# A two-block transformer on one core: engine orders from a planner of its own in place of the framework's

## The chip, the cores and the metric

The kernel runs on one core of one Trainium2 chip. A core has five instruction queues that run beside one another: TensorE (PE) for matmuls and transposes, ScalarE (ACT), VectorE (DVE), GpSimd (POOL), and SyncE (SP), which here only issues DMA transfers. Each queue is issued in the order in which the program was written out; semaphores hold an instruction back until what it needs is there. The metric is the time of one execution on the device in microseconds (us). Before the change the median of three runs is 2193.63 us (2193.45 to 2198.98).

## The reference

One sequence of 256 rows of width 1024 goes through two blocks of two layers each. All inputs are fp32.

```python
# first block, per layer
y = hybrid_mixer(x, ...)          # h = x @ w_in; three 8-head attentions (relative bias; low rank + rope; forgetting)
x = layer_norm(alpha*x + y)       # branches gated: sum_n sigmoid(g_n) * (y_n @ w_branch[n]), then @ w_out
y = memory_cross_attention(x, mem, ...);   x = layer_norm(alpha*x + y)
y = (silu(x @ w_g) * (x @ w_u)) @ w_down;  x = layer_norm(alpha*x + y)
# second block, per layer; nine vectors per layer from mod = silu(c) @ w_mod + b_mod
x = x + 0.5*g1 * swiglu(rms(x)*(1+sc1) + sh1)
x = x + g2 * mixer2(rms(x)*(1+sc2) + sh2)  # stick-breaking + dilated attention + gated linear recurrence (HGRN)
x = x + 0.5*g3 * swiglu(rms(x)*(1+sc3) + sh3)
```

The hidden width of every swiglu is 2816. Nearly all of the work is the product of 256 rows with some 300 MB of weights, read once.

## The kernel before

The 256 rows are two tiles of 128 (`t` = 0 and 1), written as two Python generators, `thread(0)` and `thread(1)`. `run` steps tile 0 until it asks for a weight, loads and splits that weight once (`weight`, L204 to L216), and hands it to tile 1 `lag` weights later. So the two tiles use the same weight a few us apart.

A weight chunk is 128x1024 fp32 (512 KB). SP loads it into one of 3 `raw` buffers (L209). ACT rounds each half to fp32r, `hi` (L214); DVE computes `lo = raw - hi` (L215). Both go into rings of 7 buffers, `wh` and `wl`, or into spare `E` buffers. Each product is three fp32r matmuls of 128x128 by 128x512 in `mm3` (L222 to L224): `xh*wh`, `xl*wh`, `xh*wl`. `wide` accumulates a group in PSUM pool `m`, one bank per tile; `narrow`, scores, transposes and the rest use pool `a`, three banks per tile. A group may start only when ACT or DVE has emptied its bank.

Results pass through small chains: transposes on PE (`blocks_T`, L267), the split of the transposed tile on ACT and DVE (L260, L261), softmax (L404 to L420: scores, row maximum on DVE, exponentials on ACT, reciprocal and product on DVE, then transposes and `values`, L391), the silu product of the FFN (L352, L353), the gate sums out of bank `m` (L539), the branch sum on GpSimd (L554), the layer norms (L289 to L296) and `modulated` with its squares on ACT (L305) and its scaling on DVE (L313). Attention is a generator beside the weights' stream (`beside`), pushed on one step per weight (`pump`).

The vectors `mod` of the second block are matrix-vector products without PE: 288 loads of 128x512 (256 KB) into 2 `mr` buffers (L753), each followed by one DVE multiply-and-sum (L754). `run` sprinkles them over the first block.

What sets the order: instructions are traced in program order, and the framework's scheduler puts each engine's into the order that is issued, by its own cost model, and gives each tile a buffer of its pool. The only hints are the lags above and `exp_next` (L171), which loads ACT's exp table right behind the last silu or sigmoid of a stage. [...]

Of the kernel before, what the change touches and what calls it, by code (L numbers as in the profile page):

```python
# [9 lines left out]
F32 = mybir.dt.float32  # L10
F32R = mybir.dt.float32r
U8 = mybir.dt.uint8
AF = mybir.ActivationFunctionType
# [103 lines left out]

class Program:
    def __init__(self, ctx, tc, io, out, probes=None):
        self.tc, self.nc, self.io, self.out, self.probes = tc, tc.nc, io, out, probes
        pool = lambda n, b, **k: ctx.enter_context(tc.tile_pool(name=n, bufs=b, **k))
# [22 lines left out]
    def tile(self, tag, shape, dt=F32):  # L147
        self.n += 1
        tag = tag if tag in self.pools else f"{tag}{self.t}"
        return self.pools[tag].tile(shape, dt, tag=tag if tag != "c" else f"c{self.n}", name=f"{tag}_{self.n}")  # L150

    def const(self, shape, ap, dt=F32):
        t = self.tile("c", shape, dt)
# [9 lines left out]
    def row(self, ap, n=D, tag=None):  # L163

        self.n += 1
        pool = self.pools["c" if tag else "bc"]
        t = pool.tile([128, n], F32, tag=tag or "bc", name=f"row_{self.n}")
        self.nc.sync.dma_start(t, ap.partition_broadcast(128))
        return t

    def exp_next(self, after):  # L171

        self.behind(self.nc.scalar.preload_act_table_set("natural_log_exp_and_others"), after)

    def behind(self, later, earlier):

        self.tc.add_manual_dep(later.ins, earlier.ins.name, mybir.DependencyInfo(
            mybir.DependencyClass.NoSync, mybir.DependencyReason.SCHED_ONLY), reason="order")

# [158 lines left out]
    def ffn(self, x, gu, dn, exps=False):  # L338

        nc = self.nc  # L340
        acc, todo = None, None
        ng = FH // 256

        def down(h, j):
            yield from self.narrow(h, range(2), dn[j * 256:j * 256 + 256], acc, j == 0, j == ng - 1)

        for j in range(ng):
            if self.t == 0:
                self.spare, self.deep, self.lag = True, NE, DEEP
            ps = yield from self.wide(x, gu[j], 512, 2)  # L350
            a = self.tile("T", [128, 512])
            silu = nc.scalar.activation(a[:, :256], ps[:, :256], AF.Silu)  # L352
# [9 lines left out]
        if self.t and exps:  # L362
            self.exp_next(silu)
        return acc


# [157 lines left out]
    def mixer(self, l, t, xT):  # L524
# [7 lines left out]
        def gates(n):  # L532
            if t == 0:
                st["bg", n] = self.row(io["b_gate"][l, n])
            out = []
            for h in range(2):
                ps = yield from self.wide(xT, main[6 + 2 * n + h], 512, 2)
                g = self.tile("S", [128, 512])
                nc.vector.tensor_tensor(g, ps, st["bg", n][:, h * 512:h * 512 + 512], op=ALU.add)  # L539
                out.append(g)  # L540
            for g in out:
                last = nc.scalar.activation(g, g, AF.Sigmoid)
            self.exp_next(last)
            return out

        def branch(n, y, gs):
# [54 lines left out]
        v = self.tile("S", [128, 8, 64])  # L601
# [329 lines left out]
    def mixer2(self, l, t, xT):  # L931
# [48 lines left out]
        def group(n):  # L980
            ps = yield from self.wide(xT, w[n], 512, 2)
            if n == 3:
                st["qs", t] = self.tile("T", [128, 512])
                silu = nc.scalar.activation(st["qs", t], ps, AF.Silu)
                if t:
                    self.exp_next(silu)
            elif n == 4:
                tasks["h"] = self.beside(hgrn_all(st["qs", t], ps))
                self.pump()
            elif n == 1:  # L990
                nc.scalar.copy(v2[:, :256], ps[:, :256])
                qd = self.normed_heads(t, ps[:, 256:], st["qg"])
                self.queries(t, self.blocks_T(qd, 2), 2, 4)
            elif n == 2:
                nc.scalar.copy(v2[:, 256:], ps[:, 256:])
                kd = self.normed_heads(t, ps[:, :256], st["kg"])
                nc.scalar.copy(k2[:, 256:], self.blocks_T(kd, 2)[:, :256])
                tasks["d"] = self.beside(dilated())
            elif n == 0:
                p = self.blocks_T(self.copied(ps), 4)  # L1000
                self.queries(t, p, 2, 0)
                nc.scalar.copy(k2[:, :256], p[:, 256:])
                tasks["s"] = self.beside(sticks())
            elif n == 5:
                st["ih", t] = self.copied(ps, "S")
            else:
                gs = self.tile("S", [128, 512])
                silu = nc.scalar.activation(gs, ps, AF.Silu)
                if t == 0 or ORDER[-1] != 6:
                    self.exp_next(silu)  # L1010
# [107 lines left out]
    def run(self, until=None):  # L1118

        self.setup()  # L1120
        ahead, behind = self.thread(0), self.thread(1)
        queue, count, passed, seen = deque(), 0, 0, 0

        def step(g, v):
            self.t = int(g is behind)
            try:
                return g.send(v)
            except StopIteration:
                return None
            finally:  # L1130
                self.t = 0

        want = step(ahead, None)
        other = None

        def follow(n):
            nonlocal other, seen
            while other is not None:
                if other[0] == "sync" and seen < passed:
                    seen += 1  # L1140
                    other = step(behind, None)
                elif other[0] == "w" and len(queue) > n:
                    ap, w = queue.popleft()
                    assert str(other[1]) == str(ap)
                    other = step(behind, w)
                else:
                    break

        while want is not None and (until is None or count < until):
            if want[0] == "sync":  # L1150
                follow(0)
                passed += 1
                want = step(ahead, None)
                continue
            w = self.weight(want[1], want[2])
            if want[0] == "w":
                queue.append((want[1], w))
            if count == 1:
                other = step(behind, None)
            if count == 8:  # L1160
                self.setup_later()
            want = step(ahead, w)
            follow(self.lag)
            count += 1
            if self.spare:
# [36 lines left out]
```

## Time and profile before

| | |
|---|---|
| median of 3 runs | 2193.63 us (2193.45 to 2198.98) |
| profiled execution | 2197.66 us, its span 2195.9 us |
| granted TensorE clock, mean | 0.996 |
| PE busy | 2105.4 us (96%), 10246 matmul records |
| DVE busy | 1576.0 us (72%) |
| ACT busy | 1232.5 us (56%) |
| DMA | 443.19 MB, 202 GB/s over the span |

Times in the views count from the start of the span. A matmul's record lasts about 0.39 us, longer than the distance to the next one's start, since matmuls are pipelined; so a PE that shows as busy can still be losing time. An idle stretch in a timeline stands in brackets, with the instruction that ended it. "PE a L267 <- DVE T L353" in the waits reads: a transpose of line 267 into pool `a` waited for the DVE instruction of line 353.

### The profile page before, as it was taken

Reading aid. Unit: us, or ns where it says so; the run is one execution under the profiler, and the core shown is the slowest. Engines: PE = TensorE matmul, PEld = TensorE weight load, DVE = VectorE, ACT = ScalarE, POOL = GpSimd, SP = SyncE. Lnnn points to the kernel's source line nnn. Section 1 sums busy time; section 2 is a strip of 40 time slices with the busy share of each in tenths; the row PEclk is TensorE's granted clock in tenths of the full one; section 3 lists DMA queues with packets and bytes.
Section 4 is the critical chain, followed back from the end, with each engine's and each line's share of the span. In section 5 each row is a group of like instructions: output and inputs, shape, how many; then the busy total and the mean of one; then the engine's idle time right before and its main releaser. Section 6 shows DMA issues by size and latency. Waiting matters only on the chain.

```text
span 2195.9 us, 29986 instructions
## 1 busy us (share of the span) xinstructions
PE 2105.4 (96%) x10246; PEld 1696.6 (77%) x10246; DVE 1576.0 (72%) x3245; ACT 1232.5 (56%) x2551; POOL 89.4 (4%) x120
## 2 busy tenths in 40 slices
PE   8999999999899999899999999999999999999999
PEld 6777777877778777788878877778887887777887
DVE  5788888777778888875585568985556556887554
ACT  5867645444476675544454446764445445776442
POOL 0000100000001011000010000000000000000000
PEclk9999999999999999999999999999999999999999
DMA  7677877888767778686656653455665665345663
GB/s 258 209 244 232 257 238 233 269 275 276 243 211 239 230 246 256 204 261 206 195 189 184 187 176 106 126 156 186 187 207 177 186 188 153 96 154 164 184 187 98
DMA packets 150320, 443.19 MB, mean 202 GB/s; under 512 B 19208, under 2 KB 24344, under 8 KB 150168
## 3 DMA queue, kind: packets, MB, share of 16 engines
q1 hardware_dynamic: 150168, 441.29, 64.2%
q8 instruction: 80, 1.31, 0.2%
q14 instruction: 72, 0.59, 0.1%
HBM read 440.10 MB, written 1.12 MB: 201 GB/s over the span
## 4 chain that ended last, share of the span: by engine, by line
PE 47%; DVE 6%; ACT 3%; DMA 2%; issue 1%; POOL 1%; POOLq 0%; ACTq 0%; DVEq 0%; SPq 0%
PE m L222 10%; PE m L223 10%; PE m L224 10%; PE a L222 5%; PE a L224 5%; PE a L223 5%; PE a L267 2%; DMA raw<-in_w_gu 1%; DVE wl L215 1%; PE a L871 1%; ACT wh L214 1%; DMA raw<-in_w_out 1%; ACT X L305 0%; POOL s L280 0%; DVE T L867 0%
## 5 line engine op out<-in xcount | busy, mean ns | idle before, releaser
L215 DVE TENSOR_TENSOR wl<-raw,wh 128x512 fp32r<-128x512 f32 (+1 forms) x982 | 654.3, 696 | 262.9 <-ACT wh L214 260.7
L214 ACT CAST wh<-raw 128x512 fp32r<-128x512 f32 (+1 forms) x982 | 568.4, 617 | 482.6 <-PE m L223 219.3
L222 PE MATMUL m<-wh,S 128*128 128x512 f32 (+2 forms) x1472 | 590.4, 401 | 20.6 <-DVE S L539 6.5
L223 PE MATMUL m<-wh,S 128*128 128x512 f32 (+2 forms) x1472 | 574.2, 390 | 3.5 <-DVE S L261 2.2
L224 PE MATMUL m<-wl,S 128*128 128x512 f32 (+2 forms) x1472 | 573.8, 391 | 0.4 <-DVE wl L215 0.4
L222 PEld LDWEIGHTS m<-wh,S 128*128 128x128 f32 x1472 | 278.6, 189 | 88.3 <-DVE S L539 9.3
L223 PEld LDWEIGHTS m<-wh,S 128*128 128x128 f32 x1472 | 279.3, 190 | 58.4 <-DVE S L325 3.9
L224 PEld LDWEIGHTS m<-wl,S 128*128 128x128 f32 x1472 | 278.0, 189 | 58.9 <-issue 2.2
L215 DVE TENSOR_TENSOR E<-raw,E 128x512 fp32r<-128x512 f32 x334 | 220.2, 687 | 123.1 <-ACT E L214 122.2
L214 ACT CAST E<-raw 128x512 fp32r<-128x512 f32 x334 | 196.0, 620 | 186.4 <-PE m L223 97.3
L754 DVE SCALAR_TENSOR_TENSOR mr<-mr,c 128x512 f32<-128x512 f32 x288 | 195.4, 689 | 108.8 <-DMA mr<-in_w_mod 107.9
L222 PE MATMUL a<-wh,S 128*128 128x512 f32 x472 | 188.8, 402 | 2.8 <-ACT S L260 2.8
L224 PE MATMUL a<-wl,S 128*128 128x512 f32 x472 | 185.9, 394 | 0.0
L223 PE MATMUL a<-wh,S 128*128 128x512 f32 x472 | 185.6, 393 | 0.0
L222 PE MATMUL m<-E,S 128*128 128x512 f32 x436 | 174.2, 400 | 0.7 <-ACT T L922 0.5
L223 PE MATMUL m<-E,S 128*128 128x512 f32 x436 | 171.8, 394 | 0.0
L224 PE MATMUL m<-E,S 128*128 128x512 f32 x436 | 171.7, 394 | 0.0
L260 ACT CAST S<-a 128x256 fp32r<-128x256 f32 (+2 forms) x200 | 85.7, 430 | 86.2 <-PE a L267 80.0
L267 PE MATMUL a<-c,T 128*128 128x128 f32 x652 | 112.2, 278 | 20.5 <-DVE T L353 6.8
L267 PEld LDWEIGHTS a<-c,T 128*128 128x128 f32 x652 | 81.2, 141 | 59.2 <-DVE T L353 12.5
L261 DVE TENSOR_TENSOR S<-a,S 128x256 fp32r<-128x256 f32 (+2 forms) x200 | 98.1, 492 | 37.8 <-ACT S L260 37.4
L222 PEld LDWEIGHTS a<-wh,S 128*128 128x128 f32 x472 | 88.5, 188 | 21.3 <-ACT S L260 3.7
(230 smaller groups left out, 2408.1 us busy)
## 6 DMA issues: line engine op xcount, KB each, us to landing
raw<-in_w_gu SPq DMA_DIRECT2D x264, 512.0 KB, 3.7
mr<-in_w_mod SPq DMA_DIRECT2D x288, 256.0 KB, 4.0
raw<-in_w_dn SPq DMA_DIRECT2D x132, 512.0 KB, 3.7
raw<-in_w_main SPq DMA_DIRECT2D x96, 512.0 KB, 4.3
raw<-in_w_in SPq DMA_DIRECT2D x56, 512.0 KB, 3.7
raw<-in_w_branch SPq DMA_DIRECT2D x24, 512.0 KB, 4.8
raw<-in_w_mo SPq DMA_DIRECT2D x16, 512.0 KB, 4.6
raw<-in_w_xkv SPq DMA_DIRECT2D x16, 512.0 KB, 4.3
```

Of the source, the lines that this page charges most:

```text
L214: nc.scalar.copy(hi[:, c], raw[:, c])
L215: nc.vector.tensor_tensor(lo[:, c], raw[:, c], hi[:, c], op=ALU.subtract)
L222: nc.tensor.matmul(ps, xh, wh, start=first, stop=False)
L223: nc.tensor.matmul(ps, xl, wh, start=False, stop=False)
L224: nc.tensor.matmul(ps, xh, wl, start=False, stop=last)
L260: nc.scalar.copy(h2, ps[:, :n])
L261: nc.vector.tensor_tensor(l2, ps[:, :n], h2, op=ALU.subtract)
L267: self.nc.tensor.transpose(ps[:, j * 128:(j + 1) * 128], src[:, j * 128:(j + 1) * 128], self.ident)
L754: nc.vector.scalar_tensor_tensor(raw, raw, 1.0, c[:, d], op0=ALU.mult, op1=ALU.mult, accum_out=m[:, k:k + 1])
L871: nc.tensor.matmul(ps[:, s], m[:, s], m[:, s], start=True, stop=True)
```

## The change

Every `nc.engine.op(...)` of the program now only records an `Op`: its engine, its data dependencies by tile and area, and a duration from a formula per engine and shape (`cost`). Pools are no longer the framework's: a `Tile` gets its place when its first instruction is placed. At the end `plan` does three things. First, each PE instruction gets as deadline (`late`) the sum of the PE durations in front of it in program order, and every other instruction the deadline of its earliest reader less its own duration and a hop; DMA gets 2500 ns and its bytes besides, and a tile that will be reused passes its next user's deadline back. Second, an event loop steps through time: a free engine takes the ready instruction with the smallest deadline, if its tiles have a free place. ACT passes over up to 11 instructions that need another function table, and loads a table when their deadline presses; `exp_next` goes away. A DMA is held until PE's progress is within 40 us of its deadline. Third, `emit` issues everything in that order, each tile at its planned place, with a semaphore on the last users of that place. The arithmetic, the tiles' sizes and the pools' counts stay.

```diff
+OVERLAP = {"PE": 0, "ACT": 95, "DVE": 83, "POOL": 0, "SP": 0}
+TABLE = 1300
+class Recorder:
+    def add(self, engine, name, args, kw):
...
+        op.dur, op.nbytes = self.cost(op, name, out[0], src, kw)
+        op.slot = max(op.dur - OVERLAP[op.eng], 40)
...
+    def cost(self, op, name, out, src, kw):
...
+        if op.eng == "PE":
+            return (4.7 + 0.4406 * n, 0) if src[1].dtype == F32R else ((1 if name == "transpose" else 2) * FP32, 0)
...
+    def plan(self):
...
+        for op in ops:
+            if op.eng == "PE":
+                op.late = total
+                total += op.slot
+        for op in reversed(ops):
+            lat = NEXT[op.eng]
+            for j in op.succ:
+                s = ops[j]
+                v = s.late - op.dur - (lat[s.eng] if s.eng != op.eng else 0)
+                if op.eng == "SP":
+                    v -= 2500 + op.nbytes / 200
+                if v < op.late:
+                    op.late = v
+            for j in reuse.get(op.i, ()):
+                if ops[j].i > op.i and ops[j].late - op.dur < op.late:
+                    op.late = ops[j].late - op.dur
...
+                    if x.eng == "SP" and early > progress:
+                        heapq.heappush(later, (early, x.i, x))
+                        continue
+                    heapq.heappush(ready[x.eng], (x.late, x.i, x))
...
+                    while q:
+                        k = heapq.heappop(q)
+                        if not room(k[2]):
+                            continue
+                        if e == "ACT" and k[2].set and table != k[2].set:
+                            held.append(k)
+                            if len(held) < 12:
+                                continue
+                            break
+                        op = k[2]
+                        break
+                    if held and (op is None or held[0][0] + TABLE < op.late):
...
+                    if e == "SP":
+                        dma = max(now + 1900, dma) + op.nbytes / 260
+                        end = dma
...
+    def emit(self, tc):
+        order, self.time = self.plan()
...
+        with tc.manual_schedule():
+            for n, op in enumerate(order):
+                while k < len(self.preload) and self.preload[k][1] <= n:
+                    self.nc.scalar.preload_act_table_set(self.preload[k][2])
...
+                ins = op.call(*args, **{a: real(v, op) for a, v in op.kw.items()})
...
 class Program:
-        self.tc, self.nc, self.io, self.out, self.probes = tc, tc.nc, io, out, probes
+        self.tc, self.nc, self.io, self.out, self.probes = tc, Recorder(tc.nc), io, out, probes
...
-    def exp_next(self, after):
-
-        self.behind(self.nc.scalar.preload_act_table_set("natural_log_exp_and_others"), after)
...
             for g in out:
-                last = nc.scalar.activation(g, g, AF.Sigmoid)
-            self.exp_next(last)
+                nc.scalar.activation(g, g, AF.Sigmoid)
...
         follow(0)
+        self.nc.emit(self.tc)
```

The orders below are each engine's, as issued. A name ends in a running number that differs between the two kernels; since every instruction is now issued by one line, the line says nothing after the change.

ScalarE at the first softmax of tile 0, before: `T_115` holds its scores, `wh_677` is a half of the next weight, `S_127` a value tile.

```order
L214 CAST wh_630<-raw_628 128x512 x2
L214 CAST wh_677<-raw_675 128x512
L415 ACT_TABLE_LOAD
L415 ACTIVATE T_115_570,s_117_572<-T_115_570,s_116_571 128x128 x4
L214 CAST wh_677<-raw_675 128x512
L450 COPY S_127_625<-m_101_505 128x512
L415 ACTIVATE T_123_607,s_125_609<-T_123_607,s_124_608 128x128 x4
L386 COPY T_134_648<-a_133_643 128x512
```

The same place after the change; here that weight is `wh_623`.

```order
L444 CAST wh_477<-raw_415 128x512
L440 ACT_TABLE_LOAD x2
L444 ACTIVATE T_115_532,s_117_572<-T_115_532,s_116_539 128x128
L444 CAST wh_578<-raw_461 128x512
L444 ACTIVATE T_115_532,s_117_572<-T_115_532,s_116_539 128x128
L444 CAST wh_578<-raw_461 128x512
L444 ACTIVATE T_115_532,s_117_572<-T_115_532,s_116_539 128x128
L444 COPY S_127_597<-m_101_437 128x512
L444 ACTIVATE T_115_532,s_117_572<-T_115_532,s_116_539 128x128
L444 CAST wh_607<-raw_474 128x512 x2
L444 ACTIVATE T_123_574,s_125_619<-T_123_574,s_124_611 128x128
L444 CAST wh_623<-raw_511 128x512
```

The rounding of that weight stood ahead of the exponentials, and now stands behind the four of `T_115`; the halves of an older weight, `wh_578`, stand between them, and two table loads in place of one in front.

TensorE at the same place, before: `a_133` takes the transposes of `T_115`, `m_110` is a group of tile 0, `m_128` one of tile 1.

```order
L223 MATMUL m_110_544<-wh_630,S_10_141 128x512
L224 MATMUL m_110_544<-wl_631,S_9_140 128x512
L267 MATMUL a_133_643<-c_117,T_115_570 128x128 x4
L222 MATMUL m_128_627<-wh_553,S_22_179 128x512
L223 MATMUL m_128_627<-wh_553,S_23_180 128x512
L224 MATMUL m_128_627<-wl_554,S_22_179 128x512
```

After the change:

```order
L444 MATMUL a_135_591<-S_99_435,E_142 128x128
L444 MATMUL m_110_501<-wl_586,S_9_173 128x512
L444 MATMUL m_128_605<-wh_452,S_22_196 128x512
L444 MATMUL m_128_605<-wh_452,S_23_205 128x512
L444 MATMUL m_128_605<-wl_466,S_22_196 128x512
L444 MATMUL m_128_605<-wh_452,S_22_196 128x512
L444 MATMUL m_128_605<-wh_452,S_23_205 128x512
L444 MATMUL m_128_605<-wl_466,S_22_196 128x512
L444 MATMUL a_135_591<-S_55_379,E_142 128x128
L444 MATMUL a_133_627<-c_131,T_115_532 128x128 x4
L444 MATMUL a_135_591<-S_99_435,E_142 128x128
L444 MATMUL m_110_501<-wh_607,S_9_173 128x512
```

The six matmuls of `m_128` stood behind the transposes and now stand ahead of them, with two score matmuls (`a_135`).

VectorE at the gates of layer 1 of the first block, before: `S_1350` is the gate sum that empties bank `m` of tile 1 (`m_1321`), `T_1343` a softmax, the `mr` rows are the sums for `mod`.

```order
L419 RECIPROCAL s_1329_5980<-s_1328_5979 128x2
L754 SCALAR_TENSOR_TENSOR mr_11396,c_3506<-mr_11396,c_3503 128x512
L420 TENSOR_TENSOR T_1326_5977<-T_1326_5977,s_1329_5980 128x512
L754 SCALAR_TENSOR_TENSOR mr_11419,c_10325<-mr_11419,c_3503 128x512
L404 SCALAR_TENSOR_TENSOR T_1343_6054<-a_1342_6049,E_5615 128x512
L754 SCALAR_TENSOR_TENSOR mr_11442,c_3506<-mr_11442,c_3503 128x512
L405 TENSOR_REDUCE s_1344_6055<-T_1343_6054 128x2
L539 TENSOR_TENSOR S_1350_6084<-m_1321_5951,row_5711 128x512
```

After the change:

```order
L444 SCALAR_TENSOR_TENSOR mr_6210,c_1090<-mr_6210,c_458 128x512
L444 SCALAR_TENSOR_TENSOR mr_6232,c_1101<-mr_6232,c_458 128x512
L444 TENSOR_TENSOR wl_6297<-raw_6196,wh_6291 128x512
L444 RECIPROCAL s_1329_6302<-s_1328_6286 128x2
L444 TENSOR_TENSOR T_1326_6244<-T_1326_6244,s_1329_6302 128x512
L444 TENSOR_TENSOR wl_6297<-raw_6196,wh_6291 128x512
L444 SCALAR_TENSOR_TENSOR T_1343_6317<-a_1342_6304,E_5592 128x512
L444 TENSOR_TENSOR wl_6324<-raw_6226,wh_6307 128x512
L444 TENSOR_REDUCE s_1344_6329<-T_1343_6317 128x2
L444 TENSOR_TENSOR wl_6324<-raw_6226,wh_6307 128x512
L444 TENSOR_TENSOR S_1350_6341<-m_1321_6219,row_5598 128x512
L444 SCALAR_TENSOR_TENSOR mr_6277,c_1090<-mr_6277,c_458 128x512
```

Three `mr` rows stood among the last seven ahead of the gate sum; now none stands among the last eight, and the nearest two come ahead of those.

ACT's function table is loaded 59 times in the order before, 47 times in the order after. The number of matmuls, transposes and transfers is the same.

## Rows read from the trace of the kernel before

**Rows 1.** Of the page: span, then engines with busy us, share of the span, instructions.

```profile
span 2195.9 us, 29986 instructions
...
PE 2105.4 (96%) x10246; PEld 1696.6 (77%) x10246; DVE 1576.0 (72%) x3245; ACT 1232.5 (56%) x2551; POOL 89.4 (4%) x120
```

**Rows 2.** Of the groups by shape on TensorE: busy us, mean ns | idle before.

```profile
L222 PE MATMUL m<-wh,S 128*128 128x512 f32 x1372 | 557.8, 407 | 17.6 <-DVE S L539 3.4 <-DVE S L324 2.8 <-ACT wh L214 2.7
...
L222 PE MATMUL a<-wh,S 128*128 128x512 f32 x472 | 188.8, 402 | 2.8 <-ACT S L260 2.8
...
L222 PE MATMUL m<-E,S 128*128 128x512 f32 x436 | 174.2, 400 | 0.7 <-ACT T L922 0.5 <-ACT T L450 0.2
...
L222 PE MATMUL a<-E,S 128*128 128x512 f32 x216 | 87.4, 405 | 0.0
...
L222 PE MATMUL m<-wh,S 128*128 128x256 f32 x68 | 19.8, 292 | 0.0
L222 PE MATMUL a<-wh,E 128*128 128x512 f32 x48 | 19.3, 402 | 0.5 <-ACT T L415 0.5
...
L222 PE MATMUL m<-wh,S 128*128 128x424 f32 x32 | 12.8, 400 | 3.0 <-DVE S L539 3.0
...
L222 PE MATMUL a<-E,E 128*128 128x512 f32 x16 | 6.2, 390 | 0.0
```

**Rows 3.** Of the timeline of TensorE, dense FFN: start us, us, what.

```profile
1714.79 0.39 PE L222 MATMUL m<-wh,S 128*128 128x512 f32 x1
...
1721.66 0.40 PE L222 MATMUL m<-wh,S 128*128 128x512 f32 x1
```

**Rows 4.** Of the timeline of TensorE, first softmax (idle before, releaser in brackets).

```profile
50.58 1.05 PE L377 MATMUL a<-S,E 128*128 128x128 f32 x8
...
58.47 0.72 PE L267 MATMUL a<-c,T 128*128 128x128 f32 x4 [4.06 <-DVE T L420]
```

**Rows 5.** Of the timeline of TensorE, the start.

```profile
4.13 1.94 PE L267 MATMUL a<-c,X 128*128 128x128 f32 x8 [4.13 <-DMA X<-in_x]
```

**Rows 6.** Of the timeline of TensorE, the end.

```profile
2190.80 0.40 PE L224 MATMUL a<-E,S 128*128 128x512 f32 x1
```

**Rows 7.** Of the stretches: us, then busy us of PE, PEld, DVE, ACT, POOL, clock, DMA.

```profile
660.00:935.00 275.00, 258.15 (x1381) 206.70 (x1381) 232.96 (x500) 169.66 (x356) 21.77 (x21) 1.00 0.74 236
...
1320.00:1485.00 165.00, 154.80 (x827) 124.27 (x826) 140.58 (x311) 114.38 (x256) 11.04 (x15) 0.99 0.44 133
1485.00:1650.00 165.00, 164.85 (x737) 133.78 (x735) 92.41 (x160) 80.75 (x162) 0.98 (x3) 1.00 0.63 192
```

**Rows 8.** Of the timeline of ScalarE, first softmax.

```profile
53.36 0.62 ACT L214 CAST wh<-raw 128x512 fp32r<-128x512 f32 x1 [6.50 <-DMA raw<-in_w_main]
53.99 1.28 ACT L415 ACT_TABLE_LOAD   x1
55.29 0.40 ACT L415 ACTIVATE T<-T,s 128x128 f32<-128x128 f32 x1
```

**Rows 9.** Of the timeline of VectorE, gates of layer 1.

```profile
645.03 0.69 DVE L754 SCALAR_TENSOR_TENSOR mr<-mr,c 128x512 f32<-128x512 f32 x1 [4.53 <-DMA mr<-in_w_mod]
```

**Rows 10.** Of the timeline of TensorE, gates of layer 1.

```profile
648.19 0.46 PE L222 MATMUL m<-wh,S 128*128 128x424 f32 x1 [3.03 <-DVE S L539]
```

**Rows 11.** Of the waits: engine, line, releaser: total us, times, longest.

```profile
DVE mr L754 <- DMA mr<-in_w_mod: 107.9, 97, 4.5
```

**Rows 12.** Of the waits of TensorE.

```profile
PE a L267 <- DVE X L313: 8.0, 10, 1.6
...
PE a L267 <- DVE X L296: 4.2, 5, 1.2
...
PE a L267 <- POOL X L554: 4.0, 4, 1.1
```

**Rows 13.** Of the page: DMA issues, KB each, median us to landing.

```profile
raw<-in_w_gu SPq DMA_DIRECT2D x264, 512.0 KB, 3.7
mr<-in_w_mod SPq DMA_DIRECT2D x288, 256.0 KB, 4.0
```

More of the change, by code (lines that the diff above doesn't have):

```diff
@@ L115, in _layout @@
     return {n: np.ascontiguousarray(a) for n, a in o.items()}
+SETS = {AF.Exp: "natural_log_exp_and_others", AF.Ln: "natural_log_exp_and_others", AF.Silu: "silu_and_others",
+        AF.Sigmoid: "sigmoid_and_others", AF.Sin: "trig_and_small"}
+NEXT = {
+    "PE": {"PE": 150, "ACT": 202, "DVE": 202, "POOL": 300, "SP": 300},
+    "ACT": {"PE": 55, "ACT": 0, "DVE": 32, "POOL": 100, "SP": 100},
+    "DVE": {"PE": 55, "ACT": 35, "DVE": 0, "POOL": 100, "SP": 100},
+    "POOL": {"PE": 60, "ACT": 40, "DVE": 35, "POOL": 0, "SP": 100},
+    "SP": {"PE": 135, "ACT": 95, "DVE": 95, "POOL": 130, "SP": 100},
+}
@@ new lines, with __init__, tile, __getattr__ @@
+class _Sketch:
+    def __init__(self):
+        import concourse.bacc as bacc
+        import concourse.tile as tile
+        self.nc = bacc.Bacc("TRN2", target_bir_lowering=False, num_devices=1)
+        self.tc = tile.TileContext(self.nc)
+        self.tc.__enter__()
+        self.pool = self.tc.alloc_tile_pool(name="sketch", bufs=1)
+    def tile(self, shape, dt, name):
+        return self.pool.tile(shape, dt, tag=name, name=name)
+class Engine:
+    def __init__(self, rec, real, name):
+        self.rec, self.real, self.name = rec, real, name
+    def __getattr__(self, op):
+        return lambda *a, **k: self.rec.add(self, op, a, k)
@@ L121, with pool @@
+FP32 = 110
 class Program:
     def __init__(self, ctx, tc, io, out, probes=None):
-        self.tc, self.nc, self.io, self.out, self.probes = tc, tc.nc, io, out, probes
-        pool = lambda n, b, **k: ctx.enter_context(tc.tile_pool(name=n, bufs=b, **k))
+        self.tc, self.nc, self.io, self.out, self.probes = tc, Recorder(tc.nc), io, out, probes
+        self.bufs = {}
+        def pool(n, b, **k):
+            self.bufs[n] = b
+            return ctx.enter_context(tc.tile_pool(name=n, bufs=1, **k))
@@ L149, in tile @@
         tag = tag if tag in self.pools else f"{tag}{self.t}"
-        return self.pools[tag].tile(shape, dt, tag=tag if tag != "c" else f"c{self.n}", name=f"{tag}_{self.n}")
+        return self.nc.tile(self.pools[tag], tag if tag != "c" else f"c{self.n}", self.bufs[tag], shape, dt, f"{tag}_{self.n}")
     def const(self, shape, ap, dt=F32):
@@ L166, in row @@
         pool = self.pools["c" if tag else "bc"]
-        t = pool.tile([128, n], F32, tag=tag or "bc", name=f"row_{self.n}")
+        t = self.nc.tile(pool, tag or "bc", 1 if tag else BUFS["bc"], [128, n], F32, f"row_{self.n}")
         self.nc.sync.dma_start(t, ap.partition_broadcast(128))
         return t
-    def exp_next(self, after):
-        self.behind(self.nc.scalar.preload_act_table_set("natural_log_exp_and_others"), after)
-    def behind(self, later, earlier):
-        self.tc.add_manual_dep(later.ins, earlier.ins.name, mybir.DependencyInfo(
-            mybir.DependencyClass.NoSync, mybir.DependencyReason.SCHED_ONLY), reason="order")
     def beside(self, gen):
@@ L351, in ffn @@
             a = self.tile("T", [128, 512])
-            silu = nc.scalar.activation(a[:, :256], ps[:, :256], AF.Silu)
+            nc.scalar.activation(a[:, :256], ps[:, :256], AF.Silu)
             nc.vector.tensor_tensor(a[:, 256:], a[:, :256], ps[:, 256:], op=ALU.mult)
@@ L361, in ffn @@
         yield from down(todo, ng - 1)
-        if self.t and exps:
-            self.exp_next(silu)
         return acc
@@ L983, in group @@
                 st["qs", t] = self.tile("T", [128, 512])
-                silu = nc.scalar.activation(st["qs", t], ps, AF.Silu)
-                if t:
-                    self.exp_next(silu)
+                nc.scalar.activation(st["qs", t], ps, AF.Silu)
             elif n == 4:
@@ L1007, in group @@
                 gs = self.tile("S", [128, 512])
-                silu = nc.scalar.activation(gs, ps, AF.Silu)
-                if t == 0 or ORDER[-1] != 6:
-                    self.exp_next(silu)
+                nc.scalar.activation(gs, ps, AF.Silu)
                 g3 = gs.rearrange("p (a b) -> p a b", a=4)
```

244 lines of the change are left out of this document (added).

## The prediction

> **What bounds the kernel now.** I read the page's busy times first. PE is busy 2105.4 of 2195.9 us, DVE and ACT far less [rows 1], so only PE's lost time can be won back by a new order. The page understates that loss, since a matmul's record overlaps the next one's. So I worked out what PE needs when nothing is late, from the groups by shape and the steps of dense stretches.
>
> In a dense FFN stretch 30 steps take 1721.66 - 1714.79 = 6.87 us: 0.229 us per 128x512 matmul [rows 3]. Of that shape line 222 issues 1372 + 472 + 436 + 216 + 48 + 16 = 2560 [rows 2]; lines 223 and 224 issue as many each, so 7680, or 1758.7 us. The 68 of 128x256 come three times too, at half a step (0.115): 23.5 us. The 32 of 128x424 at 0.19: 18.2 us. That leaves 10246 - 7680 - 204 - 96 = 2266 small records; eight of them show 1.05 us in one row, of which the last one's record is some 0.28, so 0.77 / 7 = 0.11 each [rows 4]: 249.3 us. Sum: 2049.7 us.
>
> The span is 146 us longer. PE's first work starts at 4.13 [rows 5], and 5.1 us pass from the start of the last matmul to the end [rows 6]. So 137 us are lost between steps. As idle the views show less: 2195.9 - 2105.4 = 90.5, less 4.1 and 4.7 at the ends, 81.7. The factor of 1.68 is there because each pause also hides 0.39 - 0.23 = 0.16 us of a record, and because the clock is below full for a moment after some.
>
> Then the stretches [rows 7]. In an FFN of the second block PE is idle 0.15 of 165 us: the weight stream itself costs nothing. In a mixer it is idle 10.2 of 165 us and in the mixer of layer 1 of the first block 16.9 of 275, 6% each. So the loss sits where small chains (softmax, gate sums, splits, norms) meet the weight stream, and neither DVE (85% in both) nor ACT (62% and 69%) is full there.
>
> Then two of the pauses. At 58.47 PE has been idle for 4.06 us, for a softmax product [rows 4]. ACT was idle for 6.50 us until 53.36, with the rounding of a weight whose transfer had not landed at the head of its queue; only behind it came the table load and, from 55.29, the exponentials [rows 8]. At 648.19 PE has waited 3.03 us for the gate sum that empties a bank [rows 10]. DVE had been idle for 4.53 us until 645.03, with a sum for `mod` at its head that waited for its transfer [rows 9]. Such `mod` sums held DVE 97 times for 107.9 us [rows 11]. In both places the engine that PE waits for has no lack of time; it has the wrong instruction in front.
>
> **The change part by part.** *PE's own work.* The number of matmuls, transposes and transfers stays. Each matmul record already has its own weight load (10246 and 10246 [rows 1]), so mixing groups more finely adds no load. Cost 0; I see no bound on either side but the 0.11 to 0.23 us of a step, which stays. If an accumulation that is interrupted cost anything, the present order would show it too, since the two tiles' groups already alternate.
>
> *Pauses inside stages.* Of the 81.7 us, the pauses at the tiles' edges, where a whole norm or branch sum stands between two stages, are 8.0 + 4.2 + 4.0 = 16.2 [rows 12]. The rest, 65.5 us, lies inside stages. What the new order does to them shows at the two places above. On ACT the weight's rounding now stands behind the four exponentials; on PE six matmuls of the other tile, 6 x 0.229 = 1.4 us, and two score matmuls stand where it waited. On DVE no `mod` sum stands among the eight instructions ahead of the gate sum. Bounds: all 65.5 are saved (as in the FFN with 0.15 us idle), or none. I take 65%, nearer to the FFN's row, because both places are repaired by an exchange of neighbours, and because the planner uses durations near the measured ones where the old one's cost model let a 6.5 us wait stand in front. It is not more, for two reasons. Its transfer model gives a 256 KB `mr` load 1.9 us + 262144 / 260 ns = 2.9 us, while the trace shows 4.0 [rows 13], so some of those 97 waits will come back. And the mixers' DVE stays at 85%, so an urgent instruction still finds a 0.69 us one running.
> Saved: 0.65 x 65.5 = 42.6 us of idle.
>
> *Pauses at the edges.* There the chain has a length of its own (squares, power, scaling, transposes, splits), and what helps is more of the other tile's work put in front; the two tiles are coupled by the ring of weights, which stays at 7. Bounds: 0 to 50%. I take 25%: 4 us.
>
> *Function tables.* 12 loads fewer at 1.28 us [rows 8] is 15.4 us of ACT, which is idle for 44% of the span [rows 1]; on the path I count 0. The bounds: a load that stands in front of a softmax chain delays PE by at most its 1.28 us. Four pairs of loads stand back to back in the new order, which would cost 4 x 1.28 = 5 us if each ended on the path. The trace has the first exponential 1.30 us after the start of the load [rows 8]. [...]
>
> *Transfers.* SP's queue now has `raw`, `mr` and constants sorted by deadline, weights at most 40 us ahead of it. A load's place on the path is hidden by the ring: a `raw` load lands in 3.7 us [rows 13] and feeds 12 matmuls, 2.75 us of PE, with seven buffers between. Cost 0; with the cover gone, see the second rival. *Waits added.* A reused place carries a semaphore on all of its last users. [...] I count them in the 35% that stay.
>
> *The sum.* Idle saved 42.6 + 4 = 46.6, times 1.68 = 78 us. 2197.66 - 78 = 2119.4. The profiled execution lies 4.0 us above the median of 2193.63 but inside the runs' range, so I take off 3: 2116 us. With my bounds (0 to 65.5 + 8.1) the same sum gives 2195 down to 2071.
>
> **The rivals.** *The waits only move (partial).* An order fixed by a forecast is right only while the forecast is. The underestimated `mr` loads, drifting transfers and a DVE at 85% could leave two thirds of the pauses: 0.33 x 65.5 x 1.68 = 36 us won, 2158. For it: 97 waits for `mr` transfers and 4.0 against 2.9 us. Against it: at the gates the `mr` sums are now well in front and not next to the chain.
>
> *Slower: the weight stream is late.* On SP an `mr` load that waits for its buffer holds up the `raw` loads behind it, and both wait for a DVE sum that now has a late deadline. If that eats the ring's lead, PE waits in the dense FFNs, where it now waits for nothing. Priced: 264 loads of gate and up weights [rows 13], each 0.3 us late, are 79 us; with half of my gain kept, 2195 - 39 + 79 = 2235. It decides from 0.15 us per load on, where it eats that half. Against it: `mr` loads end with the first block, and 0.15 us idle in an FFN is a wide margin. [...]
>
> *No change.* If the mixers' chains and not the queues set the pauses, a new order moves them about: 2185 to 2200. For it: 6% idle in the first and the second block alike, with and without `mr` sums. Against it: at both places that I followed, the engine that PE waited for had stood idle itself [rows 8, 9].
>
> *More than forecast.* The edges give half, the inside 90%: (59 + 8.1) x 1.68 = 113 us, 2082.
>
> **How the numbers follow.** Chances: the forecast, 2090 to 2142, 0.54; partial, 2142 to 2187, 0.22; more, below 2090, 0.12; no change 0.04; slower 0.08. The range that holds eight in ten is 2080 to 2182. A measurement of this kernel tells some 0.3% (6.6 us) from no change; by that faster has 0.54 + 0.22 + 0.12 = 0.88, the same 0.04, slower 0.08.
>
> **What would show it.** Right: PE idle in the span falls from 90.5 to about 44 us with matmul counts unchanged; DVE's waits for `mr` transfers fall well below 97 and 107.9 us; the pauses at the first softmax and at the gates of layer 1 shrink below 1 us; FFNs of the second block stay at under 1 us idle; table loads are 47. Wrong: idle that returns as PE waits for `wh` or `wl`, `mr` waits as long as before, or mixers still 6% idle; and a dense FFN whose step has grown from 0.229 us would break the floor on which all of it stands.

## The result and the profile after

The changed kernel takes 2135.28 us (median of four runs, 2133.51 to 2135.58), the kernel before 2193.54 beside it (2191.39 to 2198.98). The ratio is 0.9729, its 95% interval 0.9711 to 0.9747: 58 us faster. The forecast was 2116, with a range of 2080 to 2182.

The page after, its span and the engines' busy us (share of the span) and instructions, which answers to [rows 1]:

```profile
span 2133.5 us, 30107 instructions
...
PE 2090.6 (98%) x10246; PEld 1694.8 (79%) x10246; DVE 1571.9 (74%) x3245; ACT 1214.1 (57%) x2539; POOL 92.2 (4%) x120
```

The counts of PE and DVE are the same as before. PE is idle for 2133.5 - 2090.6 = 42.9 us, where it was 90.5.

The waits of DVE after (us in total, times, longest), which answers to [rows 11]:

```profile
DVE mr L444 <- DMA mr<-in_w_mod: 10.0, 15, 2.0
```

All recorded instructions now carry line 444, so one goes by tiles. The waits for `mr` fell from 107.9 us to 10.0.

The groups of ScalarE by line, with the function table loads:

```profile
L440 ACT ACT_TABLE_LOAD x46 | 59.0, 1283 | 0.8
L444 ACT ACT_TABLE_LOAD x1 | 1.3, 1283 | 0.7 <-PEq L1547 0.7
```

46 + 1 = 47 loads, as the order says.

The stretches after (us, then busy us of PE, PEld, DVE, ACT, POOL, clock, DMA share, GB/s), which answers to [rows 7]. The same microseconds now hold somewhat later work, so read them as mixers and FFNs, not instruction for instruction:

```profile
660.00:935.00 275.00, 269.94 (x1399) 218.24 (x1398) 229.56 (x468) 160.97 (x337) 16.47 (x12) 1.00 0.73 240
...
1320.00:1485.00 165.00, 162.80 (x842) 131.66 (x841) 130.95 (x269) 105.99 (x230) 8.77 (x10) 1.00 0.53 167
1485.00:1650.00 165.00, 164.56 (x739) 132.98 (x739) 99.43 (x175) 84.22 (x173) 2.73 (x6) 1.00 0.60 185
```

PE idle in the mixers fell from 16.9 to 5.1 and from 10.2 to 2.2 us; in the third stretch, an FFN, it went from 0.15 to 0.44.

TensorE at the first softmax after (start us, us, what; in brackets idle before and releaser), which answers to [rows 4]:

```profile
52.85 0.51 PE L444 MATMUL m<-wl,S 128*128 128x512 f32 x1 [0.66 <-DVE wl L444]
...
55.50 0.38 PE L444 MATMUL a<-S,E 128*128 128x128 f32 x2
55.72 0.60 PE L444 MATMUL a<-c,T 128*128 128x128 f32 x4
56.16 0.39 PE L444 MATMUL a<-S,E 128*128 128x128 f32 x2
```

ScalarE there, which answers to [rows 8]:

```profile
50.78 0.40 ACT L444 ACTIVATE T<-T,s 128x128 f32<-128x128 f32 x1
51.09 0.19 ACT L444 ACTIVATION_READ_ACCUMULATOR T<-T,s 128x1 f32 x1
51.55 0.58 ACT L444 COPY S<-m 128x512 f32<-128x512 f32 x1 [0.27 <-PE m L444]
52.03 0.40 ACT L444 ACTIVATE T<-T,s 128x128 f32<-128x128 f32 x1
52.33 0.19 ACT L444 ACTIVATION_READ_ACCUMULATOR T<-T,s 128x1 f32 x1
52.43 1.13 ACT L444 CAST wh<-raw 128x512 fp32r<-128x512 f32 x2
```

The transposes of the softmax (`a<-c,T`) start without a wait, where 4.06 us stood; the exponentials stand between the casts and not behind a late one. At the gates of layer 1 (612 to 632 us) the longest wait of PE is this one, where 3.03 us stood [rows 10]:

```profile
620.81 0.55 PE L444 MATMUL a<-c,T 128*128 128x128 f32 x3 [0.44 <-DVE T L444]
```

The waits of TensorE after, in total, which answers to [rows 12]:

```profile
PE m L444 <- DVE S L444: 6.7, 16, 1.5
PE m L444 <- DVE T L444: 5.6, 3, 2.5
PE a L444 <- DMA c<-in_ident: 5.4, 1, 5.4
...
PE a L444 <- POOL X L444: 0.8, 2, 0.4
...
PE m L444 <- DVE X L444: 0.3, 1, 0.3
```

The three edge rows, 16.2 us before, have shrunk to 1.1. (The 0.3 belongs to a group's start in bank `m`; transposes of `X` wait only 0.1 us in all for DVE.) The start became longer: the identity is now loaded behind the first weight and the first part of X, and PE starts at 5.44 instead of 4.13.

**Where the 62.4 us of span came from.** Take the starts of all 10246 PE records and subtract each record's dense step (0.229 for 512 columns, 0.118 for 256, 0.193 for 424, 0.110 for the small ones; 2050.6 us in all). What is left between first and last start was 136.3 us before and is 71.9 now. It has three parts:

| | before | after | saved |
|---|---|---|---|
| PE idle between records | 81.7 (127 pauses) | 32.1 (76) | 49.6 |
| overlap lost at these pauses | 21.6 | 13.5 | 8.1 |
| longer steps without idle | 33.0 | 26.3 | 6.7 |

49.6 + 8.1 + 6.7 = 64.4, less 1.3 for the later start and 0.7 at the end: 62.4. (The profiled execution of the kernel before lay 4 us above its median, so the medians differ by 58.)

The last row holds the slow clock too. Before, the granted clock reads 0.50 in five stretches at or just behind pauses (from 58.9, 550.4, 591.3, 649.4 and 1465.2 us; the second begins inside the pause that ends at 550.88), after, in three (from 357.0, 1090.9 and 1944.2). Three us of each, first before, then after (columns as above):

```profile
58.90:61.90 3.00, 3.00 (x13) 2.07 (x13) 2.29 (x6) 3.00 (x9) 0.00 (x0) 0.50 0.60 176
550.40:553.40 3.00, 2.52 (x6) 2.03 (x7) 2.79 (x9) 0.00 (x0) 0.00 (x0) 0.50 0.81 259
591.40:594.40 3.00, 3.00 (x10) 2.51 (x10) 1.59 (x4) 1.62 (x3) 0.00 (x0) 0.50 0.63 199
649.40:652.40 3.00, 3.00 (x12) 2.78 (x10) 2.41 (x6) 2.96 (x4) 0.00 (x0) 0.50 0.95 189
1465.20:1468.20 3.00, 3.00 (x8) 2.34 (x7) 2.97 (x5) 2.47 (x7) 0.64 (x1) 0.50 0.00 0
```

```profile
357.10:360.10 3.00, 3.00 (x9) 2.21 (x8) 3.00 (x7) 0.00 (x0) 0.19 (x1) 0.50 0.57 175
1090.90:1093.90 3.00, 3.00 (x9) 2.33 (x8) 1.91 (x4) 1.37 (x3) 0.00 (x0) 0.50 0.01 3
1944.30:1947.30 3.00, 3.00 (x8) 2.31 (x8) 3.00 (x7) 2.36 (x5) 0.00 (x0) 0.50 0.51 153
```

The steps without idle in them are 7.2 and 4.3 us longer than dense ones. So of the 6.7 us saved 2.8 are the clock's there, and 22.0 of the 26.3 left lie outside such stretches.

### The profile page after: what moved, and what is told of

It reads as the page before. It is cut to its first block, busy times and chain, and to the rows that moved or that the text cites. A ratio compares the mean times of both kernels' runs of the same rounds, so it can differ in the third digit from the quotient of the medians.

```text
span 2133.5 us, 30107 instructions
## 1 busy us (share of the span) xinstructions
PE 2090.6 (98%) x10246; PEld 1694.8 (79%) x10246; DVE 1571.9 (74%) x3245; ACT 1214.1 (57%) x2539; POOL 92.2 (4%) x120
## 3 DMA queue, kind: packets, MB, share of 16 engines
q8 instruction: 80, 1.31, 0.2%
## 5 line engine op out<-in xcount | busy, mean ns | idle before, releaser
L444 PE MATMUL m<-wh,S 128*128 128x512 f32 (+1 forms) x2944 | 939.4, 396 | 17.4 <-DVE S L444 6.7
L444 PE MATMUL m<-wl,S 128*128 128x512 f32 (+1 forms) x1472 | 571.7, 390 | 0.7 <-DVE wl L444 0.7
L444 PE MATMUL m<-E,S 128*128 128x512 f32 x1308 | 343.0, 397 | 2.8 <-DVE T L444 2.5
L444 PEld LDWEIGHTS m<-E,S 128*128 128x128 f32 x1308 | 243.6, 188 | 57.6 <-DVE T L444 3.0
L444 PEld LDWEIGHTS a<-wh,S 128*128 128x128 f32 x944 | 173.3, 188 | 38.3 <-DVE S L444 2.0
L444 PE MATMUL a<-E,S 128*128 128x512 f32 x648 | 181.1, 398 | 0.2 <-DVE S L444 0.2
L444 ACT CAST S<-a 128x256 fp32r<-128x256 f32 (+1 forms) x200 | 85.3, 429 | 116.0 <-PE a L444 115.1
L444 PEld LDWEIGHTS a<-E,S 128*128 128x128 f32 x648 | 119.7, 188 | 26.5 <-DVE S L444 1.1
L444 DVE TENSOR_TENSOR S<-a,S 128x256 fp32r<-128x256 f32 (+1 forms) x200 | 97.6, 490 | 38.7 <-ACT S L444 36.0
L444 PEld LDWEIGHTS a<-wl,S 128*128 128x128 f32 x472 | 88.6, 188 | 19.4 <-DVE wl L444 0.2
```

Of the source, the lines that this page charges most:

```text
L444: ins = op.call(*args, **{a: real(v, op) for a, v in op.kw.items()})
```

## The experiments

Twelve kernels, each timed beside the kernel before; ratios are to that. The first six keep the recorder and the fixed places of the changed kernel, but give some engines back the order of the kernel before. For that the planner got a table, `order_before`, and a rule on which operations are `loose`:

```diff
+        loose = lambda op: op.eng not in OLD or any(t.pool in FREE for t in op.tiles)
+        line = {e: [op for op in sorted(ops, key=lambda o: rank[o.i]) if op.eng == e and not loose(op)] for e in OLD}
...
+                    if e in OLD:
+                        nxt = line[e][at[e]] if at[e] < len(line[e]) else None
+                        if nxt is not None and nxt.i in come:
+                            come.discard(nxt.i)
+                            heapq.heappush(q, (nxt.late, nxt.i, nxt))
```

Where PE keeps its order, the deadlines are summed up along that order; of any other fixed queue they know nothing. So the kernels that fix other queues show what disagreeing queues cost, not the least that such a mixture could take. The edit also lets constants load without the 40 us limit (with DVE fixed, the `mr` and `bc` loads too), and a fixed ACT passes over nothing.

**All engines in the old order** (`all_old`).

```diff
+OLD = ('PE', 'ACT', 'DVE', 'POOL', 'SP')
+FREE = ()
```

> Recorder, fixed places and issue as in the changed kernel, but every engine gets the order of the kernel before, instruction for instruction. Theory Q (the gain comes from what stands at the head of the helper queues, DVE, ACT and SP): as the kernel before, 2185 to 2200 us, DVE's waits for mr transfers near 97 and 108 us. Theory P (the gain comes from PE's own new order): the same, 2185 to 2200. Theory F (the gain comes with the frame itself: places, semaphores, recording): 2135 to 2160.

Measured: 2199.86 us, ratio 1.0000 (0.9984 to 1.0015). DVE's waits for `mr` are there as before, as expected:

```profile
DVE mr L623 <- DMA mr<-in_w_mod: 113.0, 89, 3.9
```

So theory F falls: recorder, places and their waits cost and bring nothing that can be told, and the 58 us are the order's.

**Only the `mod` sums and their loads moved** (`mr_free`).

```diff
+OLD = ('PE', 'ACT', 'DVE', 'POOL', 'SP')
+FREE = ('mr',)
```

> As all_old, with only the 288 sums for mod on DVE, their loads on SP (and the two loads of the level masks that share their buffers) free to be placed by the planner; all else in the order of before. Theory Q: the mr waits fall under 20 us in total and the time by 15 to 30 us, to 2163 to 2180. Theory P: mr waits fall too, but the time stays within 5 us of all_old, since PE would not have had other work in front. Theory F says nothing of it.

Measured: 2216.49 us, ratio 1.0076 (1.0057 to 1.0096). Theories Q and P were both wrong. The `mr` waits halved (45.5 us), but two new pauses arose, one of them this (timeline of TensorE):

```profile
538.26 0.69 PE L623 MATMUL a<-c,T 128*128 128x128 f32 x2 [17.05 <-DVE T L623]
```

The additions that finish `mod` had kept their old place in DVE's queue. They waited there for sums now put off, and the FFN's products behind them with them. The two pauses, 17.1 and 13.4 us, are more than the loss of 17.6 us. So the kernel doesn't price the `mr` waits; it shows what one queue planned apart from another does.

**PE in the old order, the rest planned** (`pe_old`), and **PE planned, the rest in the old order** (`pe_new`).

```diff
+OLD = ('PE',)                          # pe_old
+OLD = ('ACT', 'DVE', 'POOL', 'SP')     # pe_new
```

> PE in the order of before, ACT, DVE, POOL and SP in orders that the planner works out for it. Theory Q: most of the gain stays, 2140 to 2155 us, PE idle 45 to 60 us. Theory P: most of it is gone, 2175 to 2195 us. Theory F: 2135 to 2145.

> The converse: ACT, DVE, POOL and SP in the order of before, PE in an order that the planner works out for them. Theory Q: little is won, 2175 to 2193 us, mr waits of DVE near 108 us as before. Theory P: most of the gain, 2140 to 2160 us. Theory F: 2135 to 2145.

Measured: `pe_old` 2183.96 us, ratio 0.9927 (0.9909 to 0.9945); `pe_new` 2239.53, ratio 1.0177 (1.0153 to 1.0201). Theory P's range held for the first, none for the second. The `mr` waits of DVE in the one and in the other:

```profile
DVE mr L623 <- DMA mr<-in_w_mod: 11.3, 21, 1.2
```

```profile
DVE mr L623 <- DMA mr<-in_w_mod: 108.9, 96, 3.7
```

With PE kept, the `mr` waits are nearly gone, and yet only 15 of the 58 us are won, although the deadlines follow PE's old order there. With PE alone planned the kernel loses 41 us. The parts alone add up to +26 us, together they give -58: neither the helpers' queues nor PE's order holds the gain by itself. I took from it a theory J: the gain comes only when all queues are made from one plan.

**DVE alone, and ACT alone, in the old order** (`dve_old`, `act_old`).

```diff
+OLD = ('DVE',)     # dve_old
+OLD = ('ACT',)     # act_old
```

> Only DVE keeps the order of the kernel before; PE, ACT, POOL and SP are planned around it (loads of mr and bc are not held back). Theory J (the gain comes only when all orders are made from one forecast, so one fixed engine costs most of it): 2165 to 2200 us, DVE's mr waits back above 50 us in sum. Rival V (PE's order was the one that mattered, as the kernel with PE alone kept lost 49 us; DVE can be kept at little cost): 2135 to 2160 us.

> Only ACT keeps the order of the kernel before, with the function tables in its order; the rest is planned around it. Theory J (one fixed engine costs most of the gain): 2165 to 2200 us, with the 6.50 us idle of ACT at the first softmax back. Rival V (ACT, at 57% busy, follows whatever the others do): 2135 to 2160 us.

Measured: `dve_old` 2296.02 us, ratio 1.0459 (1.0438 to 1.0480); `act_old` 2197.15, ratio 1.0014 (0.9998 to 1.0030). V falls, J's direction holds, and for DVE its size was far too small. At the first softmax of `act_old` the 6.50 us idle of ACT did not come back (1.82 was the longest there). In `dve_old` DVE's waits for `mr` are back:

```profile
DVE mr L623 <- DMA mr<-in_w_mod: 100.3, 89, 3.8
```

One fixed queue costs three quarters of the gain (PE), all of it (ACT), or more (DVE).

**All durations alike** (`flat`).

```diff
+        if op.eng in ("ACT", "DVE"):
+            op.dur = 480
```

> All engines are planned together as in the changed kernel, but every ACT and DVE instruction is counted at 480 ns, about their mean, in place of its own measured duration. Theory J (what counts is one plan for all engines, the sizes matter less): at most 15 us slower than the changed kernel, 2135 to 2150 us. Rival D (an order by forecast is worth what its durations are worth, as the prediction put it): at least half of the 58 us lost, 2165 us or more, with more pauses of PE inside the softmax and gate stages.

Measured: 2224.60 us, ratio 1.0138 (1.0119 to 1.0156). This one plan for all engines is 30 us slower than the old order by the medians. PE pauses 169 times between its records, where the changed kernel has 76. J as stated falls: one plan isn't enough, its sizes must be near. Rival D holds: it asked for half of the gain lost, and more than all of it was.

**An `mr` load counted at 0.5 us** (`mr_short`).

```diff
-                    v -= 2500 + op.nbytes / 200
+                    v -= 500 if op.tiles and op.tiles[0].pool == "mr" else 2500 + op.nbytes / 200
...
-                        end = dma
+                        end = now + 500 if op.tiles and op.tiles[0].pool == "mr" else dma
```

> The planner counts 0.5 us for an mr load, in deadline and in forecast, in place of 2.9 us, so it issues them later and places the mod sums too early. If the mod sums' waits cost what the prediction's second place suggests (a pause of PE of 3.03 us behind a DVE wait of 4.53 us), 97 waits of 1 us come back and 20 to 40 us with them: 2155 to 2175 us. Theory J: the waits come back (50 us of DVE or more), but the sums stand away from urgent work, so that 2135 to 2145 us stay.

Measured: 2558.20 us, ratio 1.1651 (1.1626 to 1.1677), far outside both. The stretch of 290 to 400 us, where PE works for 41 of 110 (columns as above):

```profile
290.00:400.00 110.00, 41.41 (x124) 29.63 (x122) 57.04 (x142) 12.75 (x24) 3.11 (x3) 0.64 0.54 169
```

The timeline in it, with SP, DVE and PE:

```profile
329.72 12.66 SPq L444 DMA_DIRECT2D mr<-in_w_mod  x8
...
333.04 0.69 DVE L444 SCALAR_TENSOR_TENSOR mr<-mr,c 128x512 f32<-128x512 f32 x1 [2.52 <-DMA mr<-in_w_mod]
...
336.75 0.69 DVE L444 SCALAR_TENSOR_TENSOR mr<-mr,c 128x512 f32<-128x512 f32 x1 [2.40 <-DMA mr<-in_w_mod]
...
340.72 0.69 DVE L444 SCALAR_TENSOR_TENSOR mr<-mr,c 128x512 f32<-128x512 f32 x1 [2.64 <-DMA mr<-in_w_mod]
...
341.95 1.29 DVE L444 TENSOR_TENSOR wl<-raw,wh 128x512 fp32r<-128x512 f32 x2
...
342.69 0.79 PE L444 MATMUL a<-wl,S 128*128 128x512 f32 x1 [20.46 <-DVE wl L444]
...
343.27 0.33 SPq L444 DMA_DIRECT2D raw<-in_w_xkv  x1
```

And the waits of SP's queue from 290 to 500 us:

```profile
SPq L444 <- DMA mr<-in_w_mod: 72.0, 63, 3.5
SPq L444 <- DVE mr L444: 63.8, 98, 1.3
```

The short count lets the plan bunch the loads (102 of the 288 in these 210 us), two at a time for two buffers. SP waits with each for a buffer, and the `raw` loads stand behind it: eight `mr` loads hold its queue for 12.66 us, and only then, at 343.27, a `raw` load is issued. ACT's longest wait for a `raw` transfer in these 210 us is 12.5 us. On DVE the weight's remainder `wl` stands behind the sums, which waited 2.52, 2.40 and 2.64 us for their transfers; `wl` then ended PE's wait of 20.46 us. This is the mechanism of the prediction's slower rival, brought about by one wrong number. The run doesn't price waits that stay away from urgent work: here the error changed the deadlines too.

**All durations at 0.8, and at 1.2, of theirs** (`scale08`, `scale12`).

```diff
+        op.dur *= 0.8 if op.eng in ("ACT", "DVE") else 1     # scale08
+        op.dur *= 1.2 if op.eng in ("ACT", "DVE") else 1     # scale12
```

> Every ACT and DVE duration in the planner is cut to 0.8 of its value; nothing else differs from the changed kernel. Theory K (an order is worth what its forecast is worth, and here the ratios between instructions stay right): between the changed kernel and the one with 480 ns for all, 2145 to 2190 us. Rival D2 (only absolute sizes set when an instruction is ready, so 20% off is as bad as no sizes): 2210 us or more. Rival N (a uniform error drops out): 2133 to 2142 us.

> The counterpart to the kernel with durations cut to 0.8: every ACT and DVE duration in the planner is multiplied by 1.2. Theory A (errors are not alike: durations counted too short put instructions at the head of a queue before their inputs are ready, and all behind them waits; durations counted too long only leave slack): at most half of the 111 us that 0.8 cost, 2140 to 2185 us. Rival D2 (20% off is 20% off, whichever way): 2210 us or more, above the kernel before.

Measured: `scale08` 2246.19 us, ratio 1.0230 (1.0206 to 1.0253); `scale12` 2155.71, ratio 0.9837 (0.9808 to 0.9865). For 0.8, D2 was right; for 1.2, theory A. Against the changed kernel, counting 20% too little costs 111 us, and 20% too much costs 20. The waits of TensorE of `scale08`:

```profile
PE a L445 <- DVE T L445: 30.1, 33, 2.5
PE a L445 <- ACT T L445: 20.7, 32, 1.4
PE a L445 <- DVE X L445: 16.2, 17, 2.1
PE m L445 <- DVE S L445: 15.6, 29, 1.4
```

And of `scale12`:

```profile
PE a L445 <- DVE T L445: 21.8, 16, 4.3
...
PE a L445 <- ACT T L445: 5.4, 8, 1.0
PE m L445 <- DVE S L445: 5.3, 8, 1.8
...
PE a L445 <- DVE X L445: 2.1, 2, 1.1
```

With the short count PE pauses 169 times for 111.4 us between its records, and the waits are spread over softmax, splits and edges alike. With the long count it pauses 69 times, less often than in the changed kernel (76), for 50.4 us. That fits theory A's reason: a consumer issued too early waits every time, one issued late finds its input there. No single pause was followed to show it.

**Two errors mended** (`fix`), and **deadlines shifted by class besides** (`climb`).

```diff
-                        end = dma
+                        end = dma + (1100 if op.tiles and op.tiles[0].pool == "mr" else 0)
...
+            if op.eng == "SP" and any(isinstance(a, bass.AP) and a.tensor.name == "in_ident" for a in op.args):
+                op.late = -1e9
...
+            op.late -= EARLIER.get((op.eng, op.name, "c" if p[0] == "c" else p.rstrip("01")), 0)     # climb alone
```

> Two errors of the forecast that the trace shows are mended: an mr load counts 4.0 us in place of 2.9, and the load of the identity, for which PE waits 5.4 us at the start, goes first on SP. Theory K: the start falls to about 4.1 us, mr waits to under 5 us in sum, and the time by 1 to 4 us, 2131 to 2134 us. Rival (no forecast of the transfers matters any more, 10 us of mr waits being off the path): 2135 us within 2 us, whatever the waits do.

> The two mendings, and deadlines shifted by class of instruction (36 classes, up to 8.6 us earlier or 4.6 us later), chosen so that the plan's own end comes 6 us earlier than with the mendings alone. Theory K: the chip follows the plan, 2124 to 2130 us. Rival O (the forecast's own error, 27 us over the span in the changed kernel, is larger than what such a shift wins): 2131 to 2142 us.

Measured: `fix` 2137.85 us, ratio 0.9732 (0.9709 to 0.9754); `climb` 2132.37, ratio 0.9713 (0.9691 to 0.9735). The `mr` waits in `fix`, and its start on TensorE:

```profile
DVE mr L447 <- DMA mr<-in_w_mod: 0.8, 2, 0.4
```

```profile
5.49 1.09 PE L447 MATMUL a<-c,X 128*128 128x128 f32 x4 [5.49 <-DMA X<-in_x]
```

The waits went as forecast, and the time did not fall (2.6 us above the changed kernel's median and just above the rival's 2133 to 2137; the intervals of the two ratios overlap): the 10 us of `mr` waits left in the changed kernel cost nothing that can be told. The start didn't move either; with the identity first, X is what comes late. `climb` has a median 2.9 us below the changed kernel's, inside rival O's range, and here too the intervals overlap. But against `fix`, timed beside it and different in the shifts alone, its runs lie apart (2131.92 to 2133.69 against 2134.56 to 2139.82): 5.5 us by the medians, where the plan gave 6. So the chip followed the plan from one to the other; that finer deadlines beat the changed kernel is not shown.

## Why the prediction was right, and where not

**The bound.** Right. PE's lost time was all there was to win: its idle fell from 90.5 to 42.9, forecast about 44. The floor held too. In a dense FFN after, 36 steps lie between these two starts on TensorE, 8.32 / 36 = 0.231 us each, against 0.229 [rows 3]:

```profile
1641.49 0.63 PE L444 MATMUL m<-wh,S 128*128 128x512 f32 x2
...
1649.81 0.62 PE L444 MATMUL a<-wh,S 128*128 128x512 f32 x2
```

**The step that failed: the factor of 1.68.** The range held, but this term was mis-sized. It divided all of the lost time by all of the idle, so it let each saved microsecond of idle take a share of the longer steps along. These 33.0 us don't hang on pauses as a whole; 26.3 of them are still there. What hangs on a pause is the overlap that it breaks, 21.6 us at 127 pauses before, 0.17 each. That is the 0.16 that the text named, and it makes a factor of (81.7 + 21.6) / 81.7 = 1.26. The other reason that it named, the clock after some pauses (0.50 in five stretches), adds the 7.2 us there: 1.35. The measured factor is 62.4 / 47.6 = 1.31. With 1.26 the forecast's own sum is 2197.66 - 46.6 x 1.26 - 3 = 2136, with 1.35 it is 2132; so this term makes 15 to 20 of the 19 us of error.

**Pauses inside stages and at edges.** Their sum, 46.6, was right (47.6 with the later start, 49.6 between records), by two errors against each other, which is luck. The edges gave 16.2 - 1.1 = 15.1 us in place of 4. The rest gave 49.6 - 15.1 = 34.5 of 65.5, 53% in place of 65%. This goes by the names of the releasers: a pause that moved from the norm to the split behind it counts as inside. At both places that were followed the pause went, as forecast.

**Function tables and transfers.** At 47 loads their share of the chain that ended last reads 0% on the page after (`ACT L440`); no experiment tried them alone. The weight stream is hardly ever late in the changed kernel (PE waits 1.5 us in all for `wh` and 0.7 for `wl`; 0.44 us idle in the FFN's stretch). The 46 loads of line 440 have 0.8 us of idle in front of them in all, and the median time from a load's end to the next ACT instruction is 0.01 us.

**The waits for `mr`.** They fell, as forecast, and the 10 us left came from the 2.9 us counted for 4.0, since they go to 0.8 when it is mended (`fix`). But neither the 97 that went nor the 15 that stayed explain the time: `pe_old` loses all but 21 of them and wins 15 us, `fix` loses all but two and wins nothing. The second place of the prediction, the gates, was a true case of this, but not the bulk.

**Why an order by deadlines brings it.** The prediction put it on durations near the measured ones, and on exchanges of neighbours in the queue. The first is borne out by `flat` (89 us above the changed kernel) and `scale08` (111 us). The second looks like too small a picture. If it were exchanges within single queues, keeping one queue should have left part of the gain: `pe_old` kept a quarter, `act_old` and `dve_old` none. That argues for queues that fit one another, but does not prove it, since the deadlines of the last two know nothing of the kept queue. The rivals: a loss by a late weight stream did not come, though `mr_short` shows that it can; the partial case, 2142 to 2187, was missed by 7 us.

What stays open: what makes the 22.0 us of longer steps outside the slow stretches (PE's own change between kinds of matmul is one candidate, not tried); how much of the loss of the kernels with a kept queue a planner that knows that queue could avoid; and what SP's and GpSimd's new orders bring, since no run kept one of them alone. ACT's idle for `raw` transfers fell from 157 to 79 us, so SP's order may have a share.

## What to carry to other kernels

When idle is turned into time, take the factor at the pauses themselves (here 81.7 us of idle, 21.6 of overlap broken at 127 pauses and 7.2 of slow clock in five stretches), not as all loss over all idle. In these kernels an instruction that waited held up those behind it in its queue (PE waited 20.46 us for DVE in `mr_short`, 17.05 in `mr_free`). An order for such queues is best made for all engines at once from measured durations, and where one is in doubt, counted rather too long: 20% too short cost 111 us here, 20% too long 20. A planned queue beside a kept one can be worse than leaving both (`pe_new` 2239.53 us, `dve_old` 2296.02).

## What the runs showed of the hardware

After a wait of 2.30 us in the changed kernel, until 355.54, more was lost than the wait itself. The stretches of TensorE read (columns as above):

```profile
352.80:356.50 3.70, 1.40 (x7) 0.84 (x6) 3.23 (x8) 0.67 (x3) 0.14 (x1) 1.00 0.87 319
356.50:360.00 3.50, 3.50 (x11) 2.59 (x10) 3.50 (x8) 0.17 (x1) 0.79 (x1) 0.58 0.49 150
366.00:372.00 6.00, 6.00 (x28) 4.87 (x27) 4.82 (x12) 2.28 (x4) 0.00 (x0) 1.00 0.78 241
```

And its timeline in between:

```profile
355.54 0.51 PE L444 MATMUL m<-wh,S 128*128 128x512 f32 x1 [2.30 <-DVE T L444]
...
356.34 0.40 PE L444 MATMUL m<-wl,S 128*128 128x512 f32 x1
356.57 0.65 PE L444 MATMUL m<-wh,S 128*128 128x512 f32 x2
357.04 0.62 PE L444 MATMUL m<-wl,S 128*128 128x512 f32 x1
357.45 1.05 PE L444 MATMUL m<-wh,S 128*128 128x512 f32 x2
358.31 0.63 PE L444 MATMUL m<-wl,S 128*128 128x512 f32 x1
358.73 1.05 PE L444 MATMUL m<-wh,S 128*128 128x512 f32 x2
359.58 0.63 PE L444 MATMUL m<-wl,S 128*128 128x512 f32 x1
```

The first matmuls after the wait still have a step of 0.23 (356.34 to 356.57). From 357.04 to 359.58 six take 2.54 us, 0.42 each, nearly double: the granted clock of the stretch reads 0.58 (0.50 from 357.10 to 360.10, as above), and by 366 it is 1.00 again. PE had no idle in these microseconds: such time stands among the "longer steps without idle", though a pause went before it. Not every such pause was followed by this. In the kernel before, the clock behind waits of 1.65, 1.77 and 1.75 us (until 344.58, 746.48 and 911.49) stayed at 1.00:

```profile
344.60:350.00 5.40, 4.83 (x38) 4.41 (x39) 4.95 (x10) 4.61 (x9) 0.00 (x0) 1.00 0.95 299
746.50:752.00 5.50, 5.50 (x37) 5.00 (x38) 5.08 (x10) 3.08 (x9) 0.00 (x0) 1.00 0.59 193
911.50:917.00 5.50, 5.50 (x28) 4.58 (x29) 3.85 (x9) 2.16 (x4) 0.00 (x0) 1.00 0.62 199
```
